# Two of the head's seven transfers issued by ScalarE, in a one-core decoder layer

## Chip, cores and metric

The kernel runs on one core of a Trainium2 chip. The core has TensorE (matmuls, with a queue of weight loads of its own), VectorE, ScalarE, GpSimd and SyncE; SyncE computes nothing and issues transfers here. Sixteen transfer engines move the data between memory and the core's on-chip buffer. The metric is the device time of one launch in microseconds (us).

## The reference

One layer of a decoder over 256 tokens of width 1024, all in float32. The mixer half computes

```python
h = rms_norm(x, pre_mix_g)
u = h @ w_in                                   # 1024 x 2560
y_a = conformer_conv_mixer(u_conf, ...)        # gate, 31-tap conv, group norm, swish
y_b = short_conv_mixer(u_sc, sconv_w)          # 3-tap conv with two gates
y_c = moba_attention(u_att)                    # 4 heads, causal, ALiBi
y_d = rglru_mixer(u_lru, ...)                  # 4-tap conv, gated recurrence, GeLU gate
x = x + rms_norm(concat(y_a, y_b, y_c, y_d) @ w_out, post_mix_g)
```

and the second half is `x + rms_norm(square(relu(rms_norm(x, pre_mlp_g) @ w1)) @ w2, post_mlp_g)` with 4096 hidden columns.

## The kernel before

Large weights come from memory in blocks of 1 MB (128 rows of 2048 columns), in the order of a list `seq`: ten for `w_in`, four for `w_out`, then sixteen each for `w1` and `w2` in turn. `load(n)` (line 107) issues block n on SyncE into one of four `raw` buffers. ScalarE makes a rounded copy `hi` of it, VectorE the rest `lo = raw - hi`, and TensorE forms each product from three matmul passes on these parts, `hi` with `hi`, `hi` with `lo` and `lo` with `hi`.

Every engine works through its instructions in the order in which the program writes them: the helper class `InOrder` (line 50) keeps this order, and the profile therefore gives line 60 for nearly everything, so that groups are told apart by their tiles. The waits between engines are put in by the framework. It also gives the transfers eight completion counters in rotation, so that the ninth transfer waits until the first has landed, and so on.

The start is special. One input array, `head`, holds for each of 128 rows some parameters (106 columns), the transposed x in eight blocks x0 to x7 of 256 columns, and the first block of `w_in` in eight blocks w0 to w7 of 256. The list `HEAD` (line 45) cuts it into seven transfers; each goes into its columns of the tile `hd` (loop in lines 142 to 146). In the texts they are h1 to h7:

| transfer | h1 | h2 | h3 | h4 | h5 | h6 | h7 |
|---|---|---|---|---|---|---|---|
| holds | parameters, x0, w0 | x1, w1 | x2, x3, w2 | x4, x5, w3 | x6, x7, w4 | w5, w6 | w7 |
| KB | 309 | 256 | 384 | 384 | 384 | 256 | 128 |

Behind them SyncE issues blocks 1 and 2 in halves, then block 3 (lines 155 to 157), then block 4.

On what has landed, VectorE scales each x block by its gain: `hf(k)` (line 211) writes `hF`, blocks 0 to 7 in order, with small operations for a parameter between them (`nl`, `ab`). ScalarE squares the x blocks in pairs (`square`, line 214; tile `sq`), computes a small exponential `e`, rounds `hF` into `hT` (`h_hi`, line 220) and loads two tables of functions, the first (Exp) in line 209, as the first thing that it does, the second (Sqrt) in line 244. TensorE, after twelve warming matmuls, multiplies block by block: `native(k)` (line 195) needs hF block k and wk, and is four matmuls in the profile. After blocks 0 to 6 it adds up the squares (`pss`, from VectorE's sum of the `sq` tiles), then takes block 7. From `pss` come `rstd`, its row `R` for all tokens (`row_of_rstd`, line 265), and the gate `cg` of the first mixer.

Of the kernel before, what the change touches and what calls it, by code (L numbers as in the profile page):

```python
# [19 lines left out]
AF = mybir.ActivationFunctionType  # L20
# [22 lines left out]
PCOLS = C_MLP + KT  # L43

HEAD = (("x0", "w0"), ("x1", "w1"), ("x2", "x3", "w2"), ("x4", "x5", "w3"), ("x6", "x7", "w4"), ("w5", "w6"), ("w7",))
HOFF = {b: PCOLS + i * S for i, b in enumerate(sum(HEAD, ()))}
HCOLS = PCOLS + 2 * KT * S

# [17 lines left out]
def hybrid_layer(ctx, tc, x, head, win, wout, w1, w2, gates, rows, out):  # L66
    nc = tc.nc
    V, A, G, T, Q = (InOrder(tc, e) for e in (nc.vector, nc.scalar, nc.gpsimd, nc.tensor, nc.sync))
# [70 lines left out]
    hd = big.tile([P, HCOLS], F32, tag="yy", name="hd")  # L139
    xs = [cst.tile([P, D], F32, name=f"x{t}") for t in range(2)]  # L140
    gw = wk.tile([P, 4, P], F32, name="gw")
    c = 0
    for blocks in HEAD:
        n = HOFF[blocks[-1]] + S
        Q.dma_start(hd[:, c:n], head[:, c:n])
        c = n

    def hb(b):
        return hd[:, HOFF[b]:HOFF[b] + S]

    def xpair(k):
        a, b = HOFF[f"x{k}"], HOFF[f"x{k + 1}"] - HOFF[f"x{k}"]
        return hd[:, a:a + 2 * b].rearrange("p (k c) -> p k c", c=b)[:, :, :S]
# [52 lines left out]
    sr = wk.tile([P, 2], F32, name="sr")  # L206
    s2 = wk.tile([P, 2], F32, name="s2")
    q = wk.tile([P, 2], F32, name="q_")
    A.preload_act_table(AF.Exp)

    def hf(k):
        V.tensor_scalar(hF[:, k, :], hb(f"x{k}"), hd[:, C_PRE + k:C_PRE + k + 1], None, op0=ALU.mult)
# [1000 lines left out]
```

## Time and profile before

| | us |
|---|---|
| median of 3 runs (lowest, highest) | 278.45 (278.35, 278.71) |
| the profiled execution | 278.95 |
| its span, first to last instruction | 277.2 |
| TensorE busy | 268.8 |
| VectorE busy | 247.9 |
| ScalarE busy | 184.4 |

The trace gives for each instruction its start from the beginning of the span, its duration and, where its engine stood idle before it, how long and what released it. For a transfer it gives the time of its issue on SyncE and the time from issue to landing. The duration of a matmul is modelled and overlaps that of its neighbours, so the distance between starts says more than the duration.

### The profile page before, as it was taken

How to read it: one execution, taken by the hardware profiler on the slowest of the kernel's cores; microseconds unless marked ns; L12 is line 12 of the kernel's file. 1: busy time of each engine (PE TensorE's matmuls, PEld its weight loads, DVE VectorE, ACT ScalarE, POOL GpSimd, SP SyncE). 2: the span in 40 equal slices, each digit the busy share in tenths (PEclk: the TensorE clock that was granted, in tenths of full speed). 3: DMA queues.
4: the chain of work that ended last, by engine and by line, in shares of the span. 5: the costliest groups of instructions: out<-in, count | busy, mean ns of one | idle time of the engine just before them, and what ended most of it. 6: DMA issues, size and time to landing. Idle time of an engine off the chain costs nothing.

```text
span 277.2 us, 4674 instructions
## 1 busy us (share of the span) xinstructions
PE 268.8 (97%) x1893; PEld 246.8 (89%) x1893; DVE 247.9 (89%) x336; ACT 184.4 (66%) x226; POOL 21.2 (8%) x53
## 2 busy tenths in 40 slices
PE   7999999999999999999999999999999999999991
PEld 5898997999987799898999999999999999999981
DVE  2889999999989998599999999999999999979165
ACT  3886659694557857878559559568577577856241
POOL 4289500000000000000000000000000000000000
PEclk9999999999999999999999999999999999999998
DMA  7998644948402735577266365375374383620004
GB/s 218 397 408 299 243 151 156 340 189 272 180 7 72 306 99 201 167 296 268 89 251 228 109 271 206 111 293 180 130 298 155 151 305 134 228 95 0 0 2 151
DMA packets 9237, 53.04 MB, mean 191 GB/s; under 512 B 1024, under 2 KB 1536, under 8 KB 3712
## 3 DMA queue, kind: packets, MB, share of 16 engines
q1 hardware_dynamic: 9216, 52.75, 51.7%
q8 instruction: 15, 0.25, 0.4%
q14 instruction: 6, 0.05, 0.0%
HBM read 51.70 MB, written 1.05 MB: 190 GB/s over the span
## 4 chain that ended last, share of the span: by engine, by line
PE 89%; DVE 4%; DMA 2%; ACT 2%; issue 1%; SPq 0%; DVEq 0%
PE pm L60 30%; PE m_acc L60 18%; PE pu L60 16%; PE acc L60 8%; PE m_sm L60 7%; PE m_mm L60 3%; DMA hd<-in_head_dram 2%; PE pz L60 2%; PE c L60 2%; DVE lo_in L60 1%; DVE u L60 1%; PE psc L60 1%; PE po L60 1%; ACT hi_in L60 1%; PE pg L60 1%
## 5 line engine op out<-in xcount | busy, mean ns | idle before, releaser
L60 DVE TENSOR_TENSOR lo_w<-raw_w,hi_w 128x2048 fp32r<-128x2048 f32 (+3 forms) x37 | 67.7, 1838 | 3.8 <-ACT hi_w L60 3.8
L60 ACT ACTIVATE hi_w<-raw_w 128x2048 fp32r<-128x2048 f32 (+2 forms) x34 | 55.1, 1663 | 1.3 <-issue 1.3
L60 PE MATMUL pm<-h2T,hi_w 128*128 128x256 f32 x240 | 32.4, 277 | 0.0
L60 PE MATMUL pm<-h2T,lo_w 128*128 128x256 f32 x240 | 32.2, 276 | 0.0
L60 PE MATMUL pm<-h2L,hi_w 128*128 128x256 f32 x240 | 32.2, 276 | 0.0
L60 ACT ACTIVATE mr<-pm 128x512 f32<-128x512 f32 x15 | 8.9, 596 | 34.1 <-PE pm L60 34.1
L60 PEld LDWEIGHTS pm<-h2T,hi_w 128*128 128x128 f32 x240 | 29.9, 188 | 0.2
L60 PEld LDWEIGHTS pm<-h2T,lo_w 128*128 128x128 f32 x240 | 29.5, 188 | 0.0
L60 PEld LDWEIGHTS pm<-h2L,hi_w 128*128 128x128 f32 x240 | 29.5, 188 | 0.0
L60 DVE SCALAR_TENSOR_TENSOR cacc<-zpad,prm,cacc 128x256 f32<-128x256 f32 x60 | 25.4, 478 | 0.1
L60 DVE TENSOR_TENSOR tl<-trs,th 128x2048 fp32r<-128x2048 f32 x11 | 25.1, 2284 | 0.0
L60 PE MATMUL m_acc<-hi_w,ml 128*128 128x512 f32 (+1 forms) x63 | 24.2, 384 | 0.0
L60 PE MATMUL m_acc<-lo_w,mh 128*128 128x512 f32 (+1 forms) x63 | 24.1, 383 | 0.0
L60 PE MATMUL m_acc<-hi_w,mh 128*128 128x512 f32 (+1 forms) x63 | 24.1, 383 | 0.0
L60 ACT ACTIVATE th<-trs 128x2048 fp32r<-128x2048 f32 x11 | 21.0, 1907 | 1.1 <-DVE trs L60 1.0
L60 PE MATMUL acc<-hi_out,yy 128*128 128x512 f32 x64 | 21.3, 401 | 0.0
L60 DVE TENSOR_TENSOR lo_in<-raw_in,hi_in 128x2048 fp32r<-128x2048 f32 (+1 forms) x11 | 20.9, 1896 | 0.2
L60 DVE TENSOR_TENSOR ml<-mf,mh 128x896 fp32r<-128x896 f32 (+3 forms) x16 | 15.4, 960 | 5.7 <-ACT mh L60 5.7
L60 ACT ACTIVATE mh<-mf 128x896 fp32r<-128x896 f32 (+3 forms) x16 | 13.6, 852 | 8.4 <-DVE mf L60 8.2
L60 PE MATMUL pu<-hT,hi_in 128*128 128x256 f32 x128 | 17.9, 282 | 0.6 <-DVE cg L60 0.6
L60 PE MATMUL pu<-hT,lo_in 128*128 128x256 f32 x128 | 17.4, 278 | 0.0
L60 ACT ACTIVATE hi_in<-raw_in 128x2048 fp32r<-128x2048 f32 (+2 forms) x12 | 17.4, 1476 | 0.0
(235 smaller groups left out, 557.9 us busy)
## 6 DMA issues: line engine op xcount, KB each, us to landing
raw_w<-in_w_dram SPq DMA_DIRECT2D x32, 1024.0 KB, 4.8
raw_in<-in_win_dram SPq DMA_DIRECT2D x7, 1024.0 KB, 5.1
raw_out<-in_wout_dram SPq DMA_DIRECT2D x4, 1024.0 KB, 5.1
raw_in<-in_win_dram SPq DMA_DIRECT2D x4, 512.0 KB, 8.0
hd<-in_head_dram SPq DMA_DIRECT2D x3, 384.0 KB, 5.9
x<-in_x_dram SPq DMA_DIRECT2D x2, 512.0 KB, 6.6
grow<-in_rows_dram SPq DMA_DIRECT2D x2, 512.0 KB, 6.7
hd<-in_head_dram SPq DMA_DIRECT2D x2, 256.0 KB, 4.9
```

Source lines behind the costliest of these rows:

```text
L60: ins = f(*args, **kwargs)
```

## The change

The loop that issues the head's transfers hands two of them to ScalarE, those that end in w3 (h4) and w6 (h6). The instruction that loads ScalarE's first table moves from line 209 to the place ahead of the loop, so that it stays ScalarE's first. Nothing else differs.

```diff
 HEAD = (("x0", "w0"), ("x1", "w1"), ("x2", "x3", "w2"), ("x4", "x5", "w3"), ("x6", "x7", "w4"), ("w5", "w6"), ("w7",))
+
+HEAD_A = ("w3", "w6")
@@
     gw = wk.tile([P, 4, P], F32, name="gw")
+    A.preload_act_table(AF.Exp)
     c = 0
     for blocks in HEAD:
         n = HOFF[blocks[-1]] + S
-        Q.dma_start(hd[:, c:n], head[:, c:n])
+        (A if blocks[-1] in HEAD_A else Q).dma_start(hd[:, c:n], head[:, c:n])
         c = n
@@
     q = wk.tile([P, 2], F32, name="q_")
-    A.preload_act_table(AF.Exp)
```

## Rows read from the trace of the kernel before

**Rows 1.** The page's busy time of each engine (us, share of the span, instructions)
```profile
PE 268.8 (97%) x1893; PEld 246.8 (89%) x1893; DVE 247.9 (89%) x336; ACT 184.4 (66%) x226; POOL 21.2 (8%) x53
```
**Rows 2.** Timeline of SyncE, 0 to 14 us: start, length, what, count
```profile
0.80 3.29 SPq L60 DMA_DIRECT2D hd<-in_head_dram  x7
4.13 5.23 SPq L60 DMA_DIRECT2D raw_in<-in_win_dram  x6
```
**Rows 3.** DMA issues in stretches of 0.5 to 4.0 us: h1, h2, h3, h5, h6
```profile
hd<-in_head_dram SPq DMA_DIRECT2D x1, 309.0 KB, 3.0
...
hd<-in_head_dram SPq DMA_DIRECT2D x1, 256.0 KB, 3.2
...
hd<-in_head_dram SPq DMA_DIRECT2D x1, 384.0 KB, 4.6
...
hd<-in_head_dram SPq DMA_DIRECT2D x1, 384.0 KB, 6.4
...
hd<-in_head_dram SPq DMA_DIRECT2D x1, 256.0 KB, 6.6
```
**Rows 4.** The chain that ended last, 0 to 30 us: start, us, what
```profile
2.16 5.88 DMA hd<-in_head_dram
```
**Rows 5.** Windows: stretch, length, PE, PEld, DVE, ACT, POOL busy, PEclk, DMA share, GB/s
```profile
4.00:5.00 1.00, 0.71 (x2) 0.62 (x3) 0.70 (x3) 0.51 (x1) 0.91 (x8) 1.00 1.03 323
5.00:6.00 1.00, 1.00 (x4) 0.82 (x3) 0.00 (x0) 0.64 (x2) 0.70 (x6) 1.00 0.86 221
...
8.00:9.00 1.00, 0.82 (x4) 0.68 (x4) 0.93 (x3) 0.94 (x2) 0.00 (x0) 1.00 1.02 375
...
12.00:22.00 10.00, 9.96 (x82) 9.65 (x83) 8.79 (x14) 8.81 (x13) 8.55 (x18) 1.00 1.01 406
...
25.50:80.00 54.50, 54.50 (x436) 51.73 (x437) 54.11 (x95) 37.10 (x52) 5.94 (x7) 1.00 0.58 209
```
**Rows 6.** Timeline of VectorE, 6 to 9 us (idle before it, and its releaser)
```profile
6.32 0.35 DVE L60 TENSOR_SCALAR hF<-hd 128x256 f32<-128x256 f32 x1 [1.42 <-DMA hd<-in_head_dram]
...
8.07 0.35 DVE L60 TENSOR_SCALAR hF<-hd 128x256 f32<-128x256 f32 x1 [1.06 <-DMA hd<-in_head_dram]
```
**Rows 7.** Timeline of TensorE and its weight loads, 0 to 30 us
```profile
4.29 3.67 PE L60 MATMUL pu<-hF,hd 128*128 128x256 f32 x12 [0.39 <-DVE hF L60]
...
8.18 3.80 PE L60 MATMUL pu<-hF,hd 128*128 128x256 f32 x16 [0.22 <-DMA hd<-in_head_dram]
...
9.12 2.46 PEld L60 LDWEIGHTS pu<-hF,hd 128*128 128x128 f32 x12 [0.24 <-DVE sq L60]
...
11.81 0.50 PE L60 MATMUL pss<-ones,sq 128*128 128x1 f32 x4
...
25.43 1.19 PE L60 MATMUL pu<-hT,hi_in 128*128 128x256 f32 x8 [0.64 <-DVE cg L60]
```
**Rows 8.** Timeline of ScalarE, 0 to 14 us
```profile
0.79 1.28 ACT L60 ACT_TABLE_LOAD   x1 [0.79 <-PEq L1205]
4.49 0.63 ACT L60 ACTIVATE sq<-hd 128x512 f32<-128x512 f32 x1 [2.42 <-DMA hd<-in_head_dram]
...
6.78 0.20 ACT L60 ACTIVATE e<-ab 128x2 f32<-128x2 f32 x1 [1.13 <-DVE ab L60]
...
8.06 0.63 ACT L60 ACTIVATE sq<-hd 128x512 f32<-128x512 f32 x1 [0.56 <-DMA hd<-in_head_dram]
...
9.75 1.28 ACT L60 ACT_TABLE_LOAD   x1
```
**Rows 9.** SyncE's own waits, 0 to 10 us: us in total, times, longest
```profile
SPq L60 <- DMA hd<-in_head_dram: 1.9, 3, 0.9
```
**Rows 10.** The page's DMA queue with data: packets, MB, share of 16 engines
```profile
q1 hardware_dynamic: 9216, 52.75, 51.7%
```
**Rows 11.** TensorE's products of the head: duration ns min/median/max, 4.2 to 5.7, 8.1 to 11.7 us
```profile
L60 PE MATMUL pu<-hF,hd x3: 634/634/797, 4.3 to 5.3; 128*128 128x256 f32 x3
...
L60 PE MATMUL pu<-hF,hd x16: 379/379/454, 8.2 to 11.6; 128*128 128x256 f32 x16
```

## The prediction, made before the changed kernel ran

> **What bounds the kernel now.** First the busy row of the page: TensorE works for 268.8 of 277.2 us [rows 1], so whatever delays its stream is paid at the end, and whatever only moves other engines is not. The profiled execution took 278.95 us with a span of 277.2, 1.75 outside the span; the median of the runs shown is 278.45, half a microsecond lower. I work out a difference on the profiled execution and add it to the median.
>
> Then the head itself, numbered h1 to h7 in order of issue. SyncE issues the seven from 0.80 us, and its first weight transfer (raw_in) goes out at 4.13, so one issue takes 3.33 / 7 = 0.48 us [rows 2]. Issue plus time to landing gives the landings [rows 2 to 4]. h1: 0.80 + 3.0 = 3.8. h2: 1.28 + 3.2 = 4.5. h3: 1.75 + 4.6 = 6.3. h4: 2.16 + 5.88 = 8.04, which is the chain's own row. h5: 2.7 + 6.4 = 9.1. h6, in the same way, about 9.8. From issue to landing the time grows from 3.0 to 6.6 us along the row: the transfers wait in a line behind each other, not for their issue. The stretches say the same: the transfer engines are busy for 1.03 and 0.86 of the two stretches from 4 to 6 us, and still for 1.01 from 12 to 22 us [rows 5]. In 5 to 6 us they are busy and yet move only 221 GB/s, against 406 from 12 to 22 us; so single packets take long there, and a longer list of requests would not be idle capacity filled.
>
> Who waits for what landed: VectorE's scaling hF number 2 (of x2, from h3) starts at 6.32 and number 4 (from h4) at 8.07, each released by the transfer [rows 6]. TensorE runs the blocks' products in block order, four matmuls each: blocks 0 to 2 from 4.29 for 3.67 us, then blocks 3 to 6 from 8.18, then the sums' product pss at 11.81 [rows 7]. So blocks 3 to 6 take 3.63 us, 0.91 a block; the twelve weight loads from 9.12 (blocks 4 to 6) take 2.46, 0.82 a block. Between 7.96 and 8.18 TensorE stood 0.22 us for h4: that is all that this engine waits for the head after its second block. In what follows it waits 0.64 us at 25.43 for VectorE's cg, at the end of a chain that began with its own transposed row, and then is full (54.50 of 54.50 us from 25.5 on) [rows 5, 7].
>
> **The change part by part.** The table load: it already is ScalarE's first instruction, from 0.79 for 1.28 us [rows 8]; moved up in the text it stays there. 0 us.
>
> ScalarE's two issues: h4 from about 2.07, h6 one issue later, 0.48 each, done near 3.0. What is queued behind them is the first Square, which started at 4.49 after 2.42 us of waiting for h2 [rows 8]. So 1.5 us cover them: 0 us. Without that cover the price would be their 0.96.
>
> SyncE's queue: two issues fewer, so h5 goes out 0.48 us earlier (near 2.2), h7 and all of raw_in 0.95 earlier. Three of its later issues waited for landings of the head, 1.9 us in all [rows 9], and will again. Earlier raw_in buys nothing by itself: the weights' first use is ScalarE's split after the squares, and no row up to 22 us names raw_in as a releaser. h4 does not go out earlier at all: 2.07 against 2.16.
>
> So issue time isn't what is won or lost; order is. Before, all transfers stood in one queue (q1 is the only one with data [rows 10]) and landed in the order in which TensorE wants them. After it h4 and h6 stand in a second queue from about 2.07 us, when most of h2 and all of h3 are still ahead in the first: h1 landed only at 3.8, h3 at 6.3. What the engines do with two queues no row shows, as there is one queue here. Two ends by rows. Best: h3 loses nothing and lands at 6.3 again. Worst: h4 and a large part of h6 go ahead of h3's last packet, and h3 lands near the place that h5 had, 9.1. Between them the nearest row is that of h4: if both queues get equal turns, h3 (384 KB and the rest of h2 before it) and h4 (384 KB) finish close together, at the time by which the sum of both had landed, 8.04. I take 8.04 for h3. h4 is then there a little sooner, which no one can use, since VectorE and TensorE take blocks 2 and 3 in order.
>
> By the Trainium skill ("DMA: Bandwidth & Descriptors", section "Queues, rings and completion order") each transfer engine goes round between the queues that have work, a packet from each; that is the way of equal turns, and the sum by it would be the one that follows, while by the rows alone either end stays open. It speaks against the change, and no run here shows it yet.
>
> The sum. Before, TensorE started block 3 at 8.18. After, h3 lands at 8.04, hF number 2 takes 0.35 us, and with 0.05 for the signals block 2 starts at 8.44. At that point TensorE is one block behind (0.82 to 0.91) and 0.26 late: +1.08 to +1.17, say +1.1. Blocks 2 to 6 then run back to back, as h5 (now near 9.8 at worst, as h6 passes it) is first needed by block 4 near 10.2. The other engines give the same: ScalarE did e and the second Square in the wait between h3 and h4; now they come after 8.04: e starts 0.46 us after hF number 2, as at 6.78 against 6.32, then 0.6 us of Square, so the Square of h4 that ran at 8.06 starts near 9.2, +1.1, and the Sqrt table load at 9.75 with it [rows 8]. Nothing behind takes this back: the splits and the transposed row start from these, the 0.64 us at 25.43 is the same chain's, and after that TensorE is full. Against the profiled execution 278.95 + 1.1 = 280.05, and against the median 278.45 + 1.1 = 279.55.
>
> **Rivals.** (a) Arrival order holds. h4 and h5 reach the engines together and share the turn that h4 had alone; h3 keeps 6.3, and h4 lands with h5 near 9.1. Block 3 starts at 9.2 instead of 8.18: +1.0, 279.45. For it: h4's issue at 2.07 is later than h3's at 1.75. Against: there is a second queue now. It differs from the forecast in the place of the gap (before block 3, not block 2), not in size.
>
> (b) Two queues cover each other's slow packets. Decisive point: h3 lands by 6.9, from where block 2 at 7.3 and five blocks of 0.9 end at 11.8 as now. Then nothing is lost, and if h4 is also early the 0.22 us before 8.18 go: 278.2 to 278.45, no slower than before. For it: the 221 GB/s of 5 to 6 us at a busy share of 0.86, so there is slow time to cover. Against: the share is still near 1 around it. Over 0.2% faster needs 0.56 us, about what this measurement can tell from no change, and the head has only 0.22 of TensorE's waiting to give; only with the 0.64 at 25.43 would it do.
>
> The Trainium skill ("Perfetto Trace Analysis", "DMA Optimizations") advises spreading issues over engines where the issuing engine's track is full and the transfers are not. Here SyncE's track is full from 0.80 to 4.13, but the transfers are full too, so the rule's condition is met by half; its case would be this rival.
>
> (c) ScalarE issues late, not at 2.07 but at 3 us or later. Then h3 is mostly through, lands near 7.2, and h4 near 8.5: block 3 at 8.6, +0.4 to +0.5, 278.9. The opposite, that ScalarE issues at once at 0.8 beside the load, so that the change does not put them behind it: then h1 waits for h4 as well, but the bytes ahead of h3 are the same; the time is that of the forecast.
>
> (d) TensorE slows down. Its first matmuls, after a pause of 0.39 us, took 634 ns, those from 8.2 on 379, at a granted clock shown as 1.00 in both stretches [rows 5, 7, 11]. If the longer pause before block 2 (6.7 to 8.4) brings the slow pace back for up to 16 matmuls, that costs 16 x 0.255 = 4 us at most, 1 to 2 more likely on top of 1.1: about 281.
>
> **How the numbers follow.** Forecast 0.46, (a) 0.12, (b) 0.27, (c) 0.11, (d) 0.04. Slower by over 0.2%: nearly all of the forecast, of (a) and (d), and 0.03 of (c), less some for a smaller size: 0.60. Faster by over 0.2%: 0.05, a corner of (b). Within 0.2%: 0.35. The range begins at (b)'s low end, 278.2, and ends where h3 lands at 8.7, that is 0.7 later than taken: 280.25. The forecast's own range is 279.2 to 280.2.
>
> **What would show it.** Right: a second queue with about 0.64 MB; hF number 2 released by the head near 8.0 instead of 6.32; TensorE idle for over 1 us before the third block's four matmuls, with twenty or so running without a break behind; pss near 12.9; the Sqrt table load near 10.9; everything from 25.43 on shifted by the same. Rival (a): hF number 2 still near 6.3 and number 4 near 9. Rival (b): hF number 2 before 6.9. Rival (c): ScalarE's issues after 3 us. Wrong altogether: pss before 11.8, or pss late and the first product of 25.43 not.

## The result, and the profile after

The changed kernel takes 280.53 us (median of 5, 280.40 to 281.89) against 278.45 for the kernel before: ratio 1.0083, 95% interval 1.0067 to 1.0099, +2.1 us by the medians, +2.3 by the ratio (1.9 to 2.8 by the interval). Slower was forecast, but by 1.1; the time lies above the range, which ended at 280.25. The profiled execution took 281.89, the slowest of the five, with a span of 280.1. Its rows may therefore show more loss than a middling execution has; in all lines of the changed kernel and its variants, L62 is what was L60.

The issues first: the timeline of both issuing engines, 0 to 15 us, against [rows 2, 8].

```profile
0.79 1.28 ACT L62 ACT_TABLE_LOAD   x1 [0.79 <-PEq L1207]
0.82 0.87 ACTq L62 DMA_DIRECT2D hd<-in_head_dram  x2
...
0.80 2.59 SPq L62 DMA_DIRECT2D hd<-in_head_dram  x5
3.43 4.78 SPq L62 DMA_DIRECT2D raw_in<-in_win_dram  x6
```

The engine's queue (ACTq) issues h4 at 0.82, 0.03 us after the table load began and 1.25 before it ended. "Behind" the load is true of the program text only. h1 was issued at 0.80, so the two went out together. What the two queues then moved is in the DMA view, 2 to 4 us (packets, MB, share of the engines); q10 is ScalarE's and wasn't there before [rows 10]:

```profile
q1 hardware_dynamic: 119, 0.28, 45.5%
q10 hardware_dynamic: 96, 0.29, 42.6%
```

They take about equal turns, and h1 pays for it. VectorE's scaling of block 0 in the kernel before, then those of blocks 0, 1 and 2 in the changed one (block 2 before: 6.32 [rows 6]):

```profile
3.79 0.45 DVE L60 TENSOR_SCALAR hF<-hd 128x256 f32<-128x256 f32 x1 [3.79 <-DMA hd<-in_head_dram]
...
4.86 0.45 DVE L62 TENSOR_SCALAR hF<-hd 128x256 f32<-128x256 f32 x1 [4.86 <-DMA hd<-in_head_dram]
6.18 0.35 DVE L62 TENSOR_SCALAR hF<-hd 128x256 f32<-128x256 f32 x1 [0.87 <-DMA hd<-in_head_dram]
...
7.41 0.35 DVE L62 TENSOR_SCALAR hF<-hd 128x256 f32<-128x256 f32 x1 [0.80 <-DMA hd<-in_head_dram]
```

By these starts h1 is 1.07 us later, h3 1.09. But the last of the seven has landed sooner, h7 at 2.94 + 5.8 = 8.7 us instead of 10.1, as the transfers no longer slow down between 4 and 6 us. The windows (last three columns: granted clock, share, GB/s), against 323 and 221 GB/s in the two halves before [rows 5]:

```profile
4.00:6.00 2.00, 0.64 (x2) 0.55 (x3) 0.45 (x1) 0.00 (x0) 1.01 (x8) 1.00 1.04 401
6.00:8.00 2.00, 2.00 (x6) 1.64 (x5) 1.02 (x5) 1.28 (x4) 1.51 (x7) 1.00 1.06 406
```

By arrival alone, TensorE should have lost far less than it did (e1 below has it: 0.41 us at pss). Its timeline says otherwise (against [rows 7]):

```profile
1.16 2.74 PE L62 MATMUL warm<-warm 128*128 128x256 bf16 x12 [1.16 <-POOL eps_r L62]
5.37 8.85 PE L62 MATMUL pu<-hF,hd 128*128 128x256 f32 x28 [1.47 <-DVE hF L62]
14.05 0.50 PE L62 MATMUL pss<-ones,sq 128*128 128x1 f32 x4
...
27.88 1.21 PE L62 MATMUL pu<-hT,hi_in 128*128 128x256 f32 x8 [1.03 <-DVE cg L62]
```

The 28 products start 1.08 us later and then run without any wait, yet take 8.68 us to pss where they took 7.52 with a wait among them. The tile view of their durations (min/median/max; 5.3 to 10.4 and 10.65 to 14 us) shows why, against [rows 11]:

```profile
L62 PE MATMUL pu<-hF,hd x12: 544/634/793, 5.4 to 10.2; 128*128 128x256 f32 x12
...
L62 PE MATMUL pu<-hF,hd x17: 379/379/544, 10.2 to 13.8; 128*128 128x256 f32 x17
```

Twelve matmuls at the slow pace instead of about four. In the slow stretch they start 0.43 us apart (twelve in 4.8 us), in the fast one 0.22. The granted clock in the two windows above reads 1.00 although both lie in the slow stretch, so the column doesn't show the change. The entries of the throttle that the trace keeps do: the first of them, full clock (the upper level of 2.4 GHz), begins at 10.54 us in the changed kernel and at 5.97 in the kernel before, in both at the place where the spacing halves. Ahead of it there is no entry, and the column counts a stretch without one as 1.00. Half the pace ahead of the entry fits the lower level of 1.2 GHz. What came before is in the first two rows: TensorE stood still for 1.47 us (0.39 before the change), from the end of the warming matmuls to the first block scaled after h1 had landed.

The delay of pss, 2.24 us, then goes through: the first product behind cg starts 2.45 later than in [rows 7], after a wait of 1.03 us instead of 0.64. The rest of the span's 2.9 us comes between 28 and 39 us, where the profiled execution's matmuls lie some 4% further apart (0.118 us instead of 0.113). The profile of e5 below has this stretch too, those of e1 and e6 don't; its cause stays open.

### The profile page after: what moved, and what is told of

Same layout as the page of the kernel before. It is cut to its first block, busy times and chain, and to the rows that moved or that the text cites. A ratio compares the mean times of both kernels' runs of the same rounds, so it can differ in the third digit from the quotient of the medians.

```text
span 280.1 us, 4674 instructions
## 1 busy us (share of the span) xinstructions
PE 270.4 (97%) x1893; PEld 248.6 (89%) x1893; DVE 248.1 (89%) x336; ACT 184.6 (66%) x226; POOL 19.5 (7%) x53
## 3 DMA queue, kind: packets, MB, share of 16 engines
HBM read 51.70 MB, written 1.05 MB: 188 GB/s over the span
## 4 chain that ended last, share of the span: by engine, by line
PE 90%; DVE 4%; ACT 2%; DMA 1%; issue 1%; DVEq 0%
PE pm L62 30%; PE pu L62 18%; PE m_acc L62 17%; PE acc L62 7%; PE m_sm L62 7%; PE m_mm L62 3%; PE pz L62 2%; PE c L62 2%; DMA hd<-in_head_dram 1%; DVE lo_in L62 1%; PE psc L62 1%; PE po L62 1%; DVE u L62 1%; ACT hi_in L62 1%; PE pg L62 1%
## 5 line engine op out<-in xcount | busy, mean ns | idle before, releaser
L62 DVE TENSOR_TENSOR lo_w<-raw_w,hi_w 128x2048 fp32r<-128x2048 f32 (+3 forms) x37 | 67.7, 1839 | 3.8 <-ACT hi_w L62 3.8
L62 ACT ACTIVATE hi_w<-raw_w 128x2048 fp32r<-128x2048 f32 (+2 forms) x34 | 55.2, 1666 | 1.3 <-issue 1.3
L62 PE MATMUL pm<-h2T,hi_w 128*128 128x256 f32 x240 | 32.4, 277 | 0.0
L62 PE MATMUL pm<-h2T,lo_w 128*128 128x256 f32 x240 | 32.2, 276 | 0.0
L62 PE MATMUL pm<-h2L,hi_w 128*128 128x256 f32 x240 | 32.2, 276 | 0.0
L62 ACT ACTIVATE mr<-pm 128x512 f32<-128x512 f32 x15 | 9.0, 597 | 33.9 <-PE pm L62 33.9
L62 PEld LDWEIGHTS pm<-h2T,hi_w 128*128 128x128 f32 x240 | 29.9, 188 | 0.2
L62 PEld LDWEIGHTS pm<-h2L,hi_w 128*128 128x128 f32 x240 | 29.5, 188 | 0.0
L62 PEld LDWEIGHTS pm<-h2T,lo_w 128*128 128x128 f32 x240 | 29.5, 188 | 0.0
L62 DVE SCALAR_TENSOR_TENSOR cacc<-zpad,prm,cacc 128x256 f32<-128x256 f32 x60 | 25.7, 486 | 0.1
L62 DVE TENSOR_TENSOR tl<-trs,th 128x2048 fp32r<-128x2048 f32 x11 | 25.1, 2286 | 0.0
L62 PE MATMUL m_acc<-hi_w,ml 128*128 128x512 f32 (+1 forms) x63 | 24.2, 384 | 0.0
L62 PE MATMUL m_acc<-lo_w,mh 128*128 128x512 f32 (+1 forms) x63 | 24.1, 383 | 0.0
L62 PE MATMUL m_acc<-hi_w,mh 128*128 128x512 f32 (+1 forms) x63 | 24.1, 383 | 0.0
L62 ACT ACTIVATE th<-trs 128x2048 fp32r<-128x2048 f32 x11 | 21.0, 1907 | 1.1 <-DVE trs L62 1.0
L62 DVE TENSOR_TENSOR lo_in<-raw_in,hi_in 128x2048 fp32r<-128x2048 f32 (+1 forms) x11 | 21.1, 1917 | 0.4 <-ACT hi_in L62 0.3
L62 PE MATMUL acc<-hi_out,yy 128*128 128x512 f32 x64 | 21.3, 401 | 0.0
L62 DVE TENSOR_TENSOR ml<-mf,mh 128x896 fp32r<-128x896 f32 (+3 forms) x16 | 15.4, 961 | 5.7 <-ACT mh L62 5.7
L62 ACT ACTIVATE mh<-mf 128x896 fp32r<-128x896 f32 (+3 forms) x16 | 13.7, 854 | 8.5 <-DVE mf L62 8.3
L62 PE MATMUL pu<-hT,hi_in 128*128 128x256 f32 x128 | 18.0, 283 | 1.0 <-DVE cg L62 1.0
L62 PE MATMUL pu<-hT,lo_in 128*128 128x256 f32 x128 | 17.5, 280 | 0.0
L62 PE MATMUL pu<-hL,hi_in 128*128 128x256 f32 x128 | 17.5, 279 | 0.0
```

The costliest lines, as they stand in the source:

```text
L62: ins = f(*args, **kwargs)
```

## The experiments

Theory P (pause): the loss is h1's lateness, and the slow pace that the pause leaves behind. Rival W (write traffic): the products run slowly because they read a tile that two queues write at 400 GB/s.

Every variant was timed beside the kernel before, whose median there was 278.81 us (e1 to e4) and 278.74 (e5 to e8). The microseconds given with a ratio are worked out from the ratio. Each kernel left one profile, of one execution.

**e1_warm19: the changed kernel with the pause filled.**

```diff
-WARM = 12
+WARM = 19
```

> The changed kernel with 19 warming matmuls instead of 12, so that TensorE doesn't stand still between 3.9 us and the landing of h1 (which comes at 4.84 in the changed kernel, 3.79 before). Theory P (pause): two terms make up the +2.1 us: h1 lands 1.08 us later because ScalarE's two transfers start at 0.82 us and take turns with it, and the pause of 1.47 us in TensorE puts off the change from the slow pace (matmuls of the head 0.43 us apart) to the fast one (0.22) from about 5.9 to 10.7 us, another 1.1. Then filling the pause gives back most of the second term: fast pace by 7 us, pss near 12.2 to 12.9, 278.8 to 279.5 us. Rival W (write traffic): the slow pace comes from the products reading the tile hd while two queues write it at 400 GB/s; more warming changes nothing: pss near 14.05, 280.5 us.

Measured: 1.0009 (0.9990 to 1.0028) of the kernel before, +0.25 us (0.55 by the medians). One constant apart from the changed kernel, and most of the loss is gone; what is left is within the noise. Its TensorE timeline:

```profile
1.16 4.23 PE L62 MATMUL warm<-warm 128*128 128x256 bf16 x19 [1.16 <-POOL eps_r L62]
5.27 7.12 PE L62 MATMUL pu<-hF,hd 128*128 128x256 f32 x28
12.22 0.50 PE L62 MATMUL pss<-ones,sq 128*128 128x1 f32 x4
```

The products start as late as in the changed kernel (5.27), with the same transfers around them, but take 6.95 us instead of 8.68. Four of them are slow, as in the kernel before. P holds, W falls. pss is 0.41 late: this is what the late arrival costs where no longer pause comes with it.

**e2_pause: the kernel before with a pause.**

```diff
-WARM = 12
+WARM = 7
```

> The kernel before (all seven transfers on SyncE) with 7 warming matmuls instead of 12, so that TensorE stands still for about 1.45 us before its first product, as in the changed kernel, but with h1 landing at 3.8 as before. Theory P: the slow pace lasts as long after the pause as in the changed kernel, to about 9.6 us; blocks 0 to 6 take 8.7 us from 4.29: pss near 12.9 instead of 11.81, +1.1 us, 279.5. Rival W: nothing changes, pss 11.8, 278.45 us.

Measured: 1.0032 (1.0011 to 1.0053), +0.9 us, without a second queue. The pause is enough:

```profile
1.16 1.68 PE L60 MATMUL warm<-warm 128*128 128x256 bf16 x7 [1.16 <-POOL eps_r L60]
4.23 8.54 PE L60 MATMUL pu<-hF,hd 128*128 128x256 f32 x28 [1.40 <-DVE hF L60]
12.61 0.50 PE L60 MATMUL pss<-ones,sq 128*128 128x1 f32 x4
```

It costs less than in the changed kernel (pss +0.80). Eleven products are slow here, and while they run, the wait for h4 that the kernel before has passes unseen; the two parts were not separated. Fewer warming matmuls are not the cause by themselves: the changed kernel has twelve and as slow a start, and e3 has twelve, a pause of 0.31 us and five slow products.

**e3_held: ScalarE's issues truly behind the table load**, the premise of the prediction.

```diff
     A.preload_act_table(AF.Exp)
+    for blk in ("x4", "w5"):
+        A.activation(hd[:, HOFF[blk]:HOFF[blk] + 1], eps_r, AF.Copy)
     c = 0
```

(`eps_r` is set ahead of it.)

> The changed kernel, but ScalarE's two issues really stand behind its table load: a one-column ScalarE copy into the first column of x4 and of w5 in hd (overwritten by the transfers) runs after the table load, and the transfers must wait for it, so they go out near 2.4 and 2.9 us. This is the case that the prediction took as given. If the prediction's model of the order is right (h3 lands at 8.04, as the sum of bytes did before), 279.5 us. If two queues also move the bytes faster, as the changed kernel's trace suggests (all seven landed by 8.8 instead of 10.1 us), h3 lands near 7 and the time is 278.5 to 278.9. h1 should land at 3.8 again and TensorE's fast pace should start near 6 us in both cases.

Measured: 1.0038 (1.0018 to 1.0058), +1.05 us (1.2 by the medians). The size forecast comes out, its place doesn't. ScalarE's queue, VectorE's scalings of blocks 2 and 4, and TensorE, from the timeline:

```profile
2.32 0.86 ACTq L62 DMA_DIRECT2D hd<-in_head_dram  x2
...
6.19 0.39 DVE L62 TENSOR_SCALAR hF<-hd 128x256 f32<-128x256 f32 x1 [0.96 <-DMA hd<-in_head_dram]
...
8.97 0.35 DVE L62 TENSOR_SCALAR hF<-hd 128x256 f32<-128x256 f32 x1 [2.07 <-DMA hd<-in_head_dram]
...
9.00 3.85 PE L62 MATMUL pu<-hF,hd 128*128 128x256 f32 x16 [0.89 <-DMA hd<-in_head_dram]
12.69 0.50 PE L62 MATMUL pss<-ones,sq 128*128 128x1 f32 x4
```

h3 lands at 6.2 as before and h4 near 8.9, just behind h5 (8.6), which SyncE had issued 0.16 us ahead of it: rival (a), arrival order, and not the equal turns of the forecast. The DMA view of the stretches 4 to 5 and 5 to 6 us:

```profile
q1 hardware_dynamic: 122, 0.32, 115.2%
...
q1 hardware_dynamic: 53, 0.15, 46.8%
q10 hardware_dynamic: 16, 0.05, 20.6%
```

The second queue moves nothing until 5 us, 2.7 us after its issue: it doesn't overtake what was issued before it. The stretch from 4 to 6 us is slow again: 261 GB/s here, 272 in the kernel before, 234 in e2. As only 16 of its packets came from the second queue, this doesn't tell what two queues at once would move.

**e4_alt17: h2, h4, h6 on ScalarE and the pause filled.**

```diff
-WARM = 12
+WARM = 17
@@
-HEAD_A = ("w3", "w6")
+HEAD_A = ("w1", "w3", "w6")
```

> ScalarE issues h2, h4 and h6, SyncE h1, h3, h5 and h7, with 17 warming matmuls. Both queues then carry the transfers in the order of use. Theory P with equal turns: h1 lands near 4.2 to 4.7, h2 with it, h3 and h4 near 6.5, all by 8.8; with the pause filled the seven blocks run from about 5.0 without a wait, at the fast pace from about 6: pss near 11.2 to 11.8, 277.8 to 278.5 us, no slower than before. Rival W: the slow pace lasts to 10 us, pss near 13.5, 280 us.

Measured: 0.9995 (0.9977 to 1.0012), the time of the kernel before; the median of 278.75 us lies a little above the range of theory P and far below the 280 of rival W. pss is 0.32 earlier in its profile:

```profile
4.89 6.76 PE L62 MATMUL pu<-hF,hd 128*128 128x256 f32 x28
11.49 0.50 PE L62 MATMUL pss<-ones,sq 128*128 128x1 f32 x4
```

**e5_h4only and e6_h6only: each part alone.**

```diff
-HEAD_A = ("w3", "w6")
+HEAD_A = ("w3",)      # e5; e6: ("w6",)
```

> One part of the change alone: ScalarE issues h4 (at 0.82 us, beside its table load, as the changed kernel's trace shows), SyncE the other six. Theory P: h4 alone already takes turns with h1 from the first packet, so h1 lands near 4.8, the pause before the first product is 1.4 us and the fast pace comes near 10.6 us: pss near 14, 280.5 us, as with both. Rival H6 (h6, which comes second on ScalarE, is what delays h2 and so the products): pss near 12.5, 279 us.

> The other part alone: ScalarE issues h6 (256 KB) at 0.82 us, SyncE the other six. Theory P: h6 takes turns with h1 in the same way, but has smaller packets (2 KB against 3 KB), so h1 lands near 4.4 to 4.6, the pause is about 1.1 us and the fast pace comes late as well: pss 13 to 14, 279.5 to 280.5 us. If a pause of 1.1 us is still short enough for the early change of pace (about 6 us), pss near 12.2, 278.8 us.

Measured: e5 1.0040 (1.0017 to 1.0062), +1.1 us; e6 1.0037 (1.0011 to 1.0064), +1.0 us. TensorE of e5, then of e6:

```profile
5.18 8.89 PE L62 MATMUL pu<-hF,hd 128*128 128x256 f32 x28 [1.28 <-DVE hF L62]
13.90 0.28 PE L62 MATMUL pss<-ones,sq 128*128 128x1 f32 x2
```

```profile
5.08 7.76 PE L62 MATMUL pu<-hF,hd 128*128 128x256 f32 x28 [1.18 <-DVE hF L62]
12.69 0.50 PE L62 MATMUL pss<-ones,sq 128*128 128x1 f32 x4
```

One transfer on ScalarE is enough to delay h1 by some 0.8 to 0.9 us and open a pause of 1.2 to 1.3; h6's turn with h2 isn't needed, so rival H6 falls. e5's profile has the full price, twelve slow products, in the slowest of its executions (281.59 us); e6's, in one of the middle (279.79), has seven, with pss between the two cases that were expected.

The times suggest that the price of the pause varies from one execution to the next. The 12 executions of e5 spread from 278.80 to 281.59, those of e6 from 278.31 to 281.38, of e2 from 279.08 to 281.15. With the pause filled the spread is 0.6 us in e1 (279.02 to 279.65) and 1.4 in e4. The kernel before, with its 0.39 us, spreads as well, by 2.7 us in 35 executions beside e1 to e4: 30 took 278.23 to 279.21, five 280.02 to 280.91. The expectation of 280.5 for e5 was right for some executions, and its median was 280.26. That slow products make these spreads is not shown, as no kernel has two profiles. The Trainium skill ("TensorE: Matmul & The Clock Gate", "What's actually happening") says that the number of slow matmuls of one kernel differs from run to run; the spreads here fit it, and no run here shows it.

**e7_alt_hold12 and e8_alt_hold15: e4 with a head start for h1**, 15 warming matmuls, meant to beat both.

```diff
-WARM = 12
+WARM = 15
@@
-HEAD_A = ("w3", "w6")
+HEAD_A = ("w1", "w3", "w6")
@@
     A.preload_act_table(AF.Exp)
+    G.memset(hd[:, HOFF["x1"]:HOFF["x1"] + 1], 0.0)   # e8: after four more memsets
```

(GpSimd's write of `warm` and, in e8, of the constants stands ahead of it; the loop of the transfers follows.)

> A version meant to beat both: ScalarE issues h2, h4 and h6, but its queue is held until about 1.2 us by a one-column GpSimd write into h2's place (overwritten by the transfer), so that h1 has a start of some 0.4 us; 15 warming matmuls fill TensorE's pause. Theory P: h1 lands near 4.0 to 4.2, first product near 4.5, then no wait: pss near 11.0 to 11.3, 277.7 to 278.1 us. If the transfers' slow stretch between 4 and 6 us (221 GB/s in the kernel before, absent where ScalarE issues at 0.82) comes back with the later issue, h3 or h4 land after 8 us and the time is 278.5 to 279.5.

> As e7, but the hold is the last of five small GpSimd writes, some 0.2 us later (ScalarE's queue from about 1.4 us). Theory P: h1 near 3.9, pss near 11.0, 277.7 to 278.1 us. If the slow stretch of 4 to 6 us depends on how late the second queue starts, it is more likely here than in e7: 278.5 to 279.5.

Measured: e7 0.9999 (0.9982 to 1.0016), e8 1.0017 (1.0002 to 1.0033). e7 does at the head what it should, pss at 11.11 and 0.70 earlier:

```profile
4.46 6.82 PE L62 MATMUL pu<-hF,hd 128*128 128x256 f32 x28
11.11 0.50 PE L62 MATMUL pss<-ones,sq 128*128 128x1 f32 x4
```

Only one product is slow in this profile instead of four; at 0.21 us each that is some 0.6 of the 0.70. Its profiled span is 276.9, 0.3 shorter than before, but no gain shows in the comparison, and the 277.7 to 278.1 expected did not come (median 278.95). In e8 the queue starts 0.25 us later than in e7 (1.42 against 1.17), and h2 lands so late that TensorE stands 1.55 us between blocks 0 and 1:

```profile
4.33 1.34 PE L62 MATMUL pu<-hF,hd 128*128 128x256 f32 x4
7.22 5.45 PE L62 MATMUL pu<-hF,hd 128*128 128x256 f32 x24 [1.55 <-DVE hF L62]
12.50 0.50 PE L62 MATMUL pss<-ones,sq 128*128 128x1 f32 x4
```

The time of e8 (median 279.29) lies in the range that was set for a slow stretch from 4 to 6 us, but there was none: 379 GB/s. The DMA issues of 1.0 to 1.6 us point to the order of issue instead. SyncE had issued h3 (384 KB) at 1.23, ahead of h2:

```profile
hd<-in_head_dram SPq DMA_DIRECT2D x1, 384.0 KB, 3.6
...
hd<-in_head_dram ACTq DMA_DIRECT2D x1, 256.0 KB, 5.3
```

h3 lands at 1.23 + 3.6 = 4.8 us, h2 at 1.42 + 5.3 = 6.7. In e7 h2 is issued 0.06 us ahead of h3 and lands at 5.2, ahead of it too. So it is in all ten kernels: the seven land in the order of their issue, whichever queue issued them.

No version tried beats the kernel before by more than the measurement can tell.

**Pause and pace, all profiles.** The pause is TensorE's idle time before its first product, the rise the first entry of full clock in the trace; a product is slow if it started before that.

| kernel | pause, us | rise at, us | slow products of 28 |
|---|---|---|---|
| before | 0.39 | 5.97 | 4 |
| changed | 1.47 | 10.54 | 12 |
| e1 | none | 6.93 | 4 |
| e2 | 1.40 | 8.78 | 11 |
| e3 | 0.31 | 6.33 | 5 |
| e4 | none | 5.84 | 2 |
| e5 | 1.28 | 10.43 | 12 |
| e6 | 1.18 | 8.07 | 7 |
| e7 | none | 4.73 | 1 |
| e8 | none | 4.80 | 1 |

The four profiles with a pause of over 1 us have the four latest rises. Within the groups the rise still differs by over 2 us (e7 and e1, e6 and the changed kernel), so a difference of a few products between two profiles, as that of e7, may be chance.

## Why the prediction was wrong

**The bound and the sign: right.** TensorE's order decides, issue time is not what is won, and what is lost at pss goes through to the end.

**The step that failed first: "h4 from about 2.07, h6 one issue later".** The trace before showed the table load's duration but not that an issue behind it has to wait, and here it didn't: 0.82. The Trainium skill ("Perfetto Trace Analysis", "DVE / Act Engine Instruction") has the sequencer ready for the next instruction as soon as it has pushed the last one into a wait queue; the trace agrees (0.82, with the load running to 2.07), and the prediction had not drawn on it. The text did name this case, under (c), and priced it as the forecast since "the bytes ahead of h3 are the same". That looked at h3 alone, which came at 7.4 and not at 8.04. The transfer that suffers is h1, by 1.07 us, and with it TensorE's first product. So the forecast's signs did not come either: TensorE stood before the first block and not before the third, and pss came at 14.05 instead of 12.9.

**The term left at nothing: TensorE's pace.** The forecast's sum has no price for it. Rival (d) had the mechanism and the time, "about 281", but set the pause before block 2 and gave it 0.04. That its time is near is luck in part: its 1.1 for the order of landing was not what arrival cost (0.41 at pss). The pause came before block 0: 0.39 became 1.47 us. Its price is shown by taking it out: e1 gives back 1.83 of the 2.24 us at pss, leaving +0.25 us on the whole.

**Equal turns, h3 at 8.04: wrong in its own case.** In e3 h3 kept 6.2 and h4 came near 8.9. Transfers shared their time where they were issued within a few hundredths of a microsecond of each other (h1 and h4 in the changed kernel, 0.02 apart, landed at 4.8 and 5.1); 0.19 us between the issues of h3 and h2 in e8 already put their landings 1.9 us apart. The sum of 1.1 came out all the same, +1.05, by rival (a)'s route: luck, as far as the forecast goes.

**Rival (b): half seen.** Where ScalarE issues at 0.82 us, in the changed kernel, all transfers land by 8.7 and the slow stretch of 4 to 6 us is gone, but h1 pays first. It isn't that two queues must move data at the time: in e5 ScalarE's one transfer had landed by 5 us, and from 5 to 6 us SyncE's queue alone moved 415 GB/s (its DMA view of that stretch):

```profile
q1 hardware_dynamic: 154, 0.41, 104.5%
```

Why the slow stretch appears only with the single queue or one that joins late (e3) stays open.

## What to carry to other kernels

The two issues that stand behind the table load in the program weren't held by it (0.82 us); what held them in e3, e7 and e8 was a write into their place that they had to wait for. So look at when a second queue really starts, and at what the first transfer needed by TensorE has to share. Before pricing a late first operand at its lateness, check whether TensorE's warm-up runs into a pause: here the late arrival cost 0.41 us at pss and the pause another 1.83. If the first operand is late anyway, warming matmuls up to its arrival are a cheap cure (by the ratio +2.3 us became +0.25).

## What was not expected of the hardware

The spread of single executions goes with the pause among the variants: 2.1 to 3.1 us where TensorE stood 1.2 to 1.4 us before its first products (e2, e5, e6), 0.6 to 1.4 where it stood 0.3 at most (e1, e3, e4, e7, e8; 12 executions each). The changed kernel (1.5 in five executions) and the kernel before (2.6 and 2.7 in 35 each) don't sort themselves by it, so this is an observation and no rule. And the transfer engines moved 396 to 415 GB/s from 4 to 6 us when both queues were issued at 0.8 us and shared the bytes (changed kernel, e1, e4), 408 and 365 with one transfer on ScalarE (e5, e6), 417 and 379 with its queue from 1.2 and 1.4 us (e7, e8), but 234 to 272 with one queue or a queue that started at 2.3 (before, e2, e3), for the same bytes.
